# A two-layer recurrent trunk: state-space rotation in PSUM, the skip term on TensorE, GpSimd's tables behind VectorE's, 12 adaLN chunks on VectorE

## The chip, the cores and the metric

The kernel runs on one core of one Trainium2 chip, as one program. The metric is the device time of one execution in microseconds. Everything is float32; the large products of the later stages are made in the fp32r form from a high and a low part of each weight.

## The reference

Two layers over a sequence of 256 tokens of width 2048. Layer 0 mixes tokens with a complex-diagonal state-space layer (S5), layer 1 with a gated recurrent block (RG-LRU); each is followed by a SwiGLU block of width 5632. Six vectors per layer (shift, scale, gate, twice) come from a conditioning vector c by the product with w_ada (adaLN).

```python
cond = silu(c)
for i in range(2):
    mod = cond @ w_ada[i] + b_ada[i]                 # 6 x 2048 numbers
    h = rmsnorm(x, norm_g[i, 0]) * (1 + sc1) + sh1
    y = s5_mixer(h) if i == 0 else rglru_mixer(h)
    x = x + g1 * y
    h = rmsnorm(x, norm_g[i, 1]) * (1 + sc2) + sh2
    x = x + g2 * swiglu(h)
return rmsnorm(x, final_g)

def s5_mixer(h):                                     # 128 groups of 16 channels, 64 complex states each
    u = h @ w_in
    a = exp((lam_re + 1j * lam_im) * dt)             # per group and state
    s[t] = a * s[t-1] + B_bar @ u[t]                 # complex, along the sequence
    y = real(C @ s) + d_skip * u                     # the skip term
    val, gate = split(gelu(y) @ w_glu)
    return val * sigmoid(gate)
```

## The kernel before

**Order.** The program is scheduled by hand: the order of the Python statements is the order on each engine's queue. Tokens are stored in an order in which four neighbours (q = 0 to 3) lie in four blocks of 64, so the scan runs over 64 blocks of four tokens.

**The stream.** All weights come through one list, `items`, into four raw buffers of 1 MB (128 x 2048 float32), loaded by SyncE's queue; `Stream.step` takes the next item and issues loads up to three items ahead, so a load waits for the release of the buffer four items back. An item of kind `f` is used as it is (the S5 input weights `win`); `w` is split by ScalarE into a high part (`wh`, L472) and by VectorE into a low part (`wl`, L487). An item of 128 adaLN columns is worked off in one of two ways, by the string `KINDS`. Kind `p`: TensorE multiplies by the conditioning vector (`ada_p`, L499, four matmuls, eight instructions, four `p` items to a PSUM bank `pa`); behind the fourth, ScalarE copies the row to SBUF (`par`, L505), and TensorE turns it into columns in `rows_out` (`pc`, L520), which are then copied to `modr` (ScalarE in the head, VectorE later). Kind `a`: one VectorE multiply with accumulation over the raw tile and the broadcast vector `cond` (`ada_a`, L491). Before, items 0 to 59 are `p` and 60 to 79 are `a`.

**The head** (`s5_layer`, until the first projection is complete): 32 adaLN items come first. Meanwhile VectorE computes the tables of the state-space layer in `prep`: the step sizes, the powers of a (`ag`, `al`), the decay `dec`, and two tables of eight rotations each (`lo`, `hi`; levels of squaring `cmul`, L164 to L168, `normalise`, L172 to L175, and the table, L249 to L259). GpSimd squares and sums for the norm, and builds with `gen_gl(t)` for a group t of eight S5 groups the matrices `gs` and `ls` (copies L274, products L279, sums L284) from `ag`, `al` and the loaded B and C. `gen2(t)` turns `gs` on TensorE into `G` (transposes L317, copy L318), multiplies `gs` by `ls` into the short convolution `pt` (L326), adds the skip term with a VectorE instruction (L328), and ScalarE copies `pt` into a Toeplitz matrix `T` (`ev`, L332). `gen_p(t)` multiplies out the rotations of a group on VectorE (L295 to L298). In program order `gen_gl(0)` and `gen_gl(1)` stand at steps 7 and 9 of the stream, the scaling of X by the norm (L886) at steps 14 to 17, `gen2(0)` and `gen2(1)` at steps 16 and 21, `gen_p` at steps 22 to 24.

**The loop** runs over t = 0 to 15. Turn t makes the projection of 128 channels on TensorE (L900, 16 k-tiles, 32 instructions) and between its k-tiles the small work of neighbouring turns: the states' inputs `pv` of t - 1 (L358), the outputs `py` of t - 2 (L395, L397), and `gen2(t + 2)`. On VectorE follow `chain` (rotate `pv`, scan, rotate back: L367 to L377) for t - 1 and `gen_p(t + 3)`; on ScalarE the copies `U` (L341), the evictions `T`, the gelu (L923) and `gen_d` (L304); on GpSimd `gen_gl(t + 4)`. When the k-tiles of a `win` item are used up, the stream steps on over the two adaLN items behind it to the next `win`.

After the loop follow the gated product of the S5 layer (`glu`), the SwiGLU block, the LRU layer and the second SwiGLU block. In the LRU layer `x0(j)` makes the products `xb`; `mac` does one k-tile of such a product, with `turn` 1 high part first, and without `turn` low part first.

Of the kernel before, what the change touches and what calls it, by code (L numbers as in the profile page):

```python
# [80 lines left out]
class S5:  # L81
# [4 lines left out]

    def __init__(self, nc, const, far, ps, lam, bcd, ident):
        self.nc, self.const, self.far, self.ps = nc, const, far, ps
        self.lam, self.bcd, self.ident = lam, bcd, ident
        self.work = None  # L90
        self.gt = {}

        def own(nm, a, b, *shape):

            return [(far if i < a else const).tile([P, *shape], F32, name=f"s5{nm}{i}") for i in range(a + b)]

        self.bct = own("bc", 4, 0, 4, 4, 16)

        self.gs = own("gs", 2, 0, 4, 2, 4, 32)

        self.G = own("G", 2, 2, 2, 4, 128) * 4

        self.ls0 = l = own("ls", 2, 4, 4, 2, 5, 32)
        self.ls = [l[i] for i in (0, 1, 2, 3, 4, 5, 0, 1, 2, 3, 4, 5, 0, 2, 3, 4)]

        p = own("pt", 3, 2, 4, 2, 64)
        self.pt = [p[i] for i in (0, 1, 2, 3, 4, 0, 1, 2, 3, 4, 0, 1, 2, 3, 4, 3)]

        self.T0 = t = own("T", 2, 3, 4, 4, 32)
        self.T = 3 * t + [t[2]]  # L110
        self.d0 = own("d0", 0, 2, 8, 64)

    def load(self, w):
        self.lam_t = w.tile([P, 3, 64], F32, name="s5lam")
        self.dsk = self.const.tile([P, 64], F32, name="s5dsk")
        self.nc.sync.dma_start(self.lam_t, self.lam[:, 0:3])
        self.nc.sync.dma_start(self.dsk, self.lam[:, 3])

# [4 lines left out]
    def prep(self, w):  # L123
# [10 lines left out]
        self.ag, self.al, self.lo, self.hi = ag, al, lo, hi  # L134
        self.id4 = c.tile([P, 32], F32, name="s5id")
        for x in self.gs + self.ls0 + self.d0 + self.T0:
            nc.gpsimd.memset(x, 0.0)
        for q in range(4):
            v.tensor_copy(self.id4[32 * q:32 * q + 32], self.ident[32 * q:32 * q + 32, 32 * q:32 * q + 32])

# [64 lines left out]
        cmul(a4, a2, a2)  # L205
        v.tensor_scalar(ag[:, :, 0], ag[:, :, 2], -1.0, None, MUL)
        yield
# [33 lines left out]
        for lev in range(2):  # L241
# [13 lines left out]
            if lev == 0:  # L255
                cmul(e2, p4, p4)
                normalise(e2)
                base = e2
        v.tensor_scalar(hi[:, :, 0], hi[:, :, 2], -1.0, None, MUL)  # L259

    def gen_gl(self, t):
# [44 lines left out]
    def gen2(self, t):  # L306
# [13 lines left out]
        def tt():  # L320

            pt = self.ps.tile([P, 4, 32], F32, tag="pt", bufs=1, name=f"pt{t}")
            tp.append(pt)
            for i in range(2):
                for r in range(4):
                    nc.tensor.matmul(pt[32 * r:32 * r + 32], gs[:, r, i, 3], ls[:, r, i, 0:4], start=(i == 0),  # L326
                                     stop=(i == 1), tile_position=(0, 32 * r), skip_group_check=True)
            nc.vector.scalar_tensor_tensor(pt[:, 0], self.id4, self.dsk[:, 4 * t:4 * t + 1], pt[:, 0], MUL, ADD)  # L328

# [14 lines left out]
    def states(self, t):  # L344
# [15 lines left out]
        def chain():  # L360
            vv, d0 = st["pv"], self.d0[t % 2]

            def wt(nm):
                return w.tile([P, 4, 2, 64], F32, tag=nm, bufs=1, name=f"{nm}_{t}")
            m, n = wt("sm"), wt("sn")
            co, si = (bc(pt[:, :, i], 2, 2) for i in range(2))
# [3 lines left out]
            v.tensor_tensor(m[:, :, 1], m[:, :, 1], n[:, :, 0], SUB)  # L370
            v.tensor_tensor_scan(n.rearrange("p r i n -> p (r i n)"), d0.rearrange("p a n -> p (a n)"),
                                 m.rearrange("p r i n -> p (r i n)"), 0.0, MUL, ADD)
            S = w.tile([P, 4, 2, 64], F32, tag="S", bufs=2, name=f"S_{t}")
            v.tensor_tensor(m, n, si, MUL)
            v.tensor_tensor(S, n, co, MUL)
            v.tensor_tensor(S[:, :, 0], S[:, :, 0], m[:, :, 1], SUB)
# [31 lines left out]
class Stream:  # L408
# [105 lines left out]
    def rows_out(self):  # L514

        if self.rows:
            nc, (rows, n) = self.nc, self.rows
            pc = self.ps.tile([P, 4], F32, tag="pc", bufs=1, name=f"pc{n}")
            for j in range(4):
                nc.tensor.matmul(pc[:, j:j + 1], rows[:, j * P:j * P + P], self.ones, start=True, stop=True)  # L520
            self.cols(self.mod[:, n - 3:n + 1], pc)
            self.rows = None
# [53 lines left out]
class Model:  # L576
# [250 lines left out]
    def s5_layer(self):  # L827
# [3 lines left out]
        with ExitStack() as c:  # L831
# [3 lines left out]
            far = tc.tile_pool(name="s5far", bufs=1, side="right")  # L835
            s5 = S5(nc, const, far.__enter__(), s5ps, d["s5lam"], d["s5bc"], self.ident)
            hf = const.tile([P, 16, T], F32, name="s5h")
# [17 lines left out]
            with tc.tile_pool(name="s5prep", bufs=1) as pw:  # L855
# [9 lines left out]
                stat = self.norm_stat(mm, "s5")  # L865
                for i in range(14):
                    st.step()
# [5 lines left out]
                    if 1 <= i < 4:  # L873
                        for k in range(6 * i - 6, min(6 * i, 16)):
                            self.sq_add(k, nc.gpsimd)
                    if i in (7, 9):
                        s5.gen_gl((i - 7) // 2)
                for _ in prep:
                    pass
            next(stat, None)  # L880
            s5.work = c.enter_context(tc.tile_pool(name="s5w", bufs=1))
            for i in range(14, 28):
                st.step()
                if i < 18:
                    for k in range(4 * i - 56, 4 * i - 52):
                        nc.vector.tensor_tensor(self.X[:, k], self.X[:, k], self.rs, MUL)  # L886
                if i in (16, 21):
                    for f in s5.gen2((i - 16) // 5):
                        f()
                    s5.gen_gl((i - 16) // 5 + 2)  # L890
                if 22 <= i < 25:
                    s5.gen_p(i - 22)
            st.late = True
# [164 lines left out]
    def lru_layer(self):  # L1058
        nc, tc, d = self.nc, self.tc, self.d
        v, s, e = nc.vector, nc.scalar, nc.gpsimd  # L1060
        with ExitStack() as c:
# [112 lines left out]
            def x0(j):  # L1174
                if j > 1:
                    first.append(self.product(ps, self.rhs_h, 16, f"xb{j}", "evict", (1,) if j % 4 == 2 else ()))

# [59 lines left out]
    def run(self):  # L1237
# [50 lines left out]
        items += ada(12, 16) + ada(28, 29) + win[0:1] + ada(29, 32)  # L1288
        items += mix(win[1:], ada(32, 60), 2)
        items += mix(wglu, ada(60, 80), 2, 3, 2) + gu[0][0][:2] + ada(80, 84) + mix(gu[0][0][2:], ada(84, 96), 1, 3)  # L1290
# [9 lines left out]
        self.st.ps = ctx.enter_context(tc.tile_pool(name="side", bufs=1, space=PSUM))  # L1300
        self.st.ew = const
        self.s5_layer()
        self.ps = ctx.enter_context(tc.tile_pool(name="mm", bufs=4, space=PSUM))
# [26 lines left out]

KINDS = "p" * 60 + "a" * 20 + "qqqp" + "a" * 56 + "qqqp" + "a" * 32 + "qqqp" + "a" * 12

# [13 lines left out]
def lay_out(i):  # L1346
# [37 lines left out]
    ldt = np.broadcast_to(i["s5_log_dt"][0][:, None], (P, 64))  # L1384
    dsk = np.repeat(i["s5_d"][0].reshape(16, P).T, 4, axis=1)
    o["s5lam"] = np.stack([states(i["s5_lam_re"][0]), states(i["s5_lam_im"][0]), states(ldt), dsk], 1)
# [43 lines left out]
```

## Time and profile before

| | |
|---|---|
| time, median of 3 runs | 2495.81 us (2494.57 to 2498.04) |
| the profiled execution's own time | 2500.8 us |
| its span, granted clock | 2499.0 us, 0.976 |
| PE busy, PEld busy | 2379.5 us (95%), 2045.1 us (82%) |
| DVE, ACT, POOL busy | 1895.4 us (76%), 1298.4 us (52%), 339.3 us (14%) |
| read from HBM | 614.57 MB, 247 GB/s over the span |

PE is TensorE's matmul, PEld its weight load, DVE is VectorE, ACT ScalarE, POOL GpSimd, SP SyncE. L12 is line 12 of the kernel. A line of the timeline has the start and the length in us, the engine, the line of the kernel, the operation, out<-in and a count, and in brackets the idle time before it and what ended it. A group has its busy time, the mean of one instruction in ns, and the idle time of the engine just before its instructions. Matmuls are pipelined and their ends modelled, so that a busy PE need not be PE at its peak.

### The profile page before, as it was taken

Reading aid. Unit: us, or ns where it says so; the run is one execution under the profiler, and the core shown is the slowest. Engines: PE = TensorE matmul, PEld = TensorE weight load, DVE = VectorE, ACT = ScalarE, POOL = GpSimd, SP = SyncE. Lnnn points to the kernel's source line nnn. Section 1 sums busy time; section 2 is a strip of 40 time slices with the busy share of each in tenths; the row PEclk is TensorE's granted clock in tenths of the full one; section 3 lists DMA queues with packets and bytes.
Section 4 is the critical chain, followed back from the end, with each engine's and each line's share of the span. In section 5 each row is a group of like instructions: output and inputs, shape, how many; then the busy total and the mean of one; then the engine's idle time right before and its main releaser. Section 6 shows DMA issues by size and latency. Waiting matters only on the chain. (4 is left out here: it accounts for less than half of the span.)

```text
span 2499.0 us, 37144 instructions
## 1 busy us (share of the span) xinstructions
PE 2379.5 (95%) x14374; PEld 2045.1 (82%) x14374; DVE 1895.4 (76%) x2618; ACT 1298.4 (52%) x2525; POOL 339.3 (14%) x345
## 2 busy tenths in 40 slices
PE   5389998999999999999999898999999999999998
PEld 1167787887888888888888787888788888888887
DVE  9857757888776887777989999898777555555565
ACT  1257785456455444444456765554645444444443
POOL 5558730001000000000002332010100000000000
PEclk8689998999999999999999999999999999999999
DMA  9465555887666898776985446879776456555453
GB/s 374 184 237 211 211 211 224 325 321 284 251 255 236 287 337 314 291 296 241 326 319 195 149 169 236 331 273 334 282 299 253 171 186 215 202 187 198 168 191 135
DMA packets 98416, 619.07 MB, mean 248 GB/s; under 512 B 11200, under 2 KB 15680, under 8 KB 38976
## 3 DMA queue, kind: packets, MB, share of 16 engines
q1 hardware_dynamic: 96368, 613.04, 66.7%
q10 hardware_dynamic: 1872, 3.67, 0.4%
q8 instruction: 112, 1.84, 0.3%
q14 instruction: 64, 0.52, 0.1%
HBM read 614.57 MB, written 2.10 MB: 247 GB/s over the span
## 5 line engine op out<-in xcount | busy, mean ns | idle before, releaser
L487 DVE TENSOR_TENSOR wl<-raw,wh 128x1024 fp32r<-128x1024 f32 (+2 forms) x824 | 887.0, 1099 | 337.6 <-ACT wh L472 335.2
L472 ACT ACTIVATE wh<-raw 128x1024 fp32r<-128x1024 f32 (+2 forms) x824 | 768.4, 952 | 659.6 <-PE d L605 186.8
L605 PE MATMUL u<-H,wh 128*128 128x512 f32 x1376 | 472.0, 389 | 0.0
L605 PE MATMUL d<-hid,wh 128*128 128x512 f32 x1376 | 469.3, 389 | 0.0
L605 PE MATMUL g<-H,wh 128*128 128x512 f32 x1328 | 455.7, 389 | 0.0
L604 PE MATMUL d<-hid,wl 128*128 128x256 f32 x1376 | 380.1, 276 | 0.0
L604 PE MATMUL u<-H,wl 128*128 128x256 f32 x1376 | 379.8, 276 | 0.0
L604 PE MATMUL g<-H,wl 128*128 128x256 f32 x1328 | 366.7, 276 | 0.0
L605 PEld LDWEIGHTS u<-H,wh 128*128 128x128 f32 x1376 | 258.3, 188 | 53.6
L605 PEld LDWEIGHTS d<-hid,wh 128*128 128x128 f32 x1376 | 258.3, 188 | 53.1
L605 PEld LDWEIGHTS g<-H,wh 128*128 128x128 f32 x1328 | 249.3, 188 | 50.8
L491 DVE CUSTOM_DVE_ANT_0 raw<-raw,cond 128x2048 f32<-128x2048 f32 x120 | 274.7, 2290 | 3.6 <-DMA raw<-in_wada 3.6
L604 PEld LDWEIGHTS d<-hid,wl 128*128 128x128 f32 x1376 | 258.3, 188 | 0.6
L604 PEld LDWEIGHTS u<-H,wl 128*128 128x128 f32 x1376 | 258.3, 188 | 0.0
L604 PEld LDWEIGHTS g<-H,wl 128*128 128x128 f32 x1328 | 249.2, 188 | 0.9
L499 PE MATMUL pa<-raw,condz 128*32 128x512 f32 x576 | 87.5, 714 | 70.7 <-ACT par L505 45.6
L900 PE MATMUL in<-s5h,raw 128*128 128x256 f32 x512 | 145.1, 401 | 1.3 <-ACT s5h L854 1.3
L793 ACT ACTIVATE gs<-gs 128x256 f32<-128x256 f32 x88 | 36.7, 418 | 202.8 <-DVE gs L642 202.8
L605 PE MATMUL lg<-H,wh 128*128 128x512 f32 x340 | 118.1, 394 | 0.0
L605 PE MATMUL xb<-H,wh 128*128 128x512 f32 x315 | 110.9, 395 | 0.0
L499 PEld LDWEIGHTS pa<-raw,condz 128*32 128x32 f32 x576 | 14.8, 118 | 110.9 <-ACT par L505 52.8
L900 PEld LDWEIGHTS in<-s5h,raw 128*128 128x128 f32 x512 | 87.9, 195 | 19.6 <-issue 11.1
(419 smaller groups left out, 3761.3 us busy)
## 6 DMA issues: line engine op xcount, KB each, us to landing
raw<-in_wada SPq DMA_DIRECT2D x192, 1024.0 KB, 6.0
raw<-in_gu SPq DMA_DIRECT2D x176, 1024.0 KB, 4.8
raw<-in_dn SPq DMA_DIRECT2D x128, 704.0 KB, 4.2
raw<-in_lruin SPq DMA_DIRECT2D x44, 1024.0 KB, 5.0
raw<-in_s5glu SPq DMA_DIRECT2D x32, 1024.0 KB, 6.2
raw<-in_lruout SPq DMA_DIRECT2D x32, 704.0 KB, 5.6
raw<-in_s5win SPq DMA_DIRECT2D x16, 1024.0 KB, 8.5
raw<-in_lruri SPq DMA_DIRECT2D x8, 512.0 KB, 5.4
```

The costliest lines, as they stand in the source:

```text
L472: nc.scalar.activation(dh, src, AF.Copy)
L487: self.nc.vector.tensor_tensor(*self.lazy.pop(0), SUB)
L491: self.nc.vector.tensor_tensor_reduce(t, t, self.cond, 1.0, 0.0, MUL, ADD, self.mod[:, n:n + 1])
L499: nc.tensor.matmul(self.bank[32 * c:32 * c + 32], self.condz[:, 4 * q + c], t[:, 512 * c:512 * c + 512], start=(q == 0), stop=(q == 3), ti ...
L604: mm(bank[:, 0], wl, x[:, 0], start=first, stop=False, skip_group_check=True)
L605: mm(bank, wh, x, start=False, stop=last, skip_group_check=True)
L793: nc.scalar.activation(g, g, AF.Silu)
L900: nc.tensor.matmul(bank, st.next()[0], hf[:, k], start=(k == 0), stop=(k == 15))
```

## The change

It has five parts. (1) `gen_gl(0)` and `gen_gl(1)` follow all of `prep`, `gen2(0)` and `gen2(1)` move to steps 23 and 27 of the stream, `gen_p` to steps 23 to 25, the scaling of X to steps 16 to 19; three negations of tables move to the end of `prep`. (2) The skip term is a table `skip` (identity blocks times `d_skip`, 128 x 512, built once by VectorE), and TensorE adds it to `pt` with four small matmuls against the identity; L328 goes. `pt` moves into one PSUM bank with `pc`, (3) which makes room for a bank `px`: `chain` keeps its product m there instead of in SBUF, and the scan writes over `pv` in PSUM. (4) adaLN items 48 to 59 become kind `a`; behind each of the `win` items 1 to 12 now stand one `p` and one `a`, behind 13 and 14 two `p`. (5) All `xb` products take the first k-tile high part first, not only every fourth.

```diff
@@ S5.load, S5.prep @@
-        self.dsk = self.const.tile([P, 64], F32, name="s5dsk")
+        self.dsk = w.tile([P, 16], F32, name="s5dsk")
...
+        self.skip = self.far.tile([P, 16, 32], F32, name="s5skip")
...
+        v.tensor_tensor(self.skip, bc(id4, 1, 16), bc(self.dsk, 2, 32), MUL)
...
-        v.tensor_scalar(ag[:, :, 0], ag[:, :, 2], -1.0, None, MUL)
...
-        v.tensor_scalar(al[:, :, 2], al[:, :, 0], -1.0, None, MUL)
...
         v.tensor_scalar(hi[:, :, 0], hi[:, :, 2], -1.0, None, MUL)
+        v.tensor_scalar(ag[:, :, 0], ag[:, :, 2], -1.0, None, MUL)
+        v.tensor_scalar(al[:, :, 2], al[:, :, 0], -1.0, None, MUL)
@@ S5.gen2, tt @@
-            pt = self.ps.tile([P, 4, 32], F32, tag="pt", bufs=1, name=f"pt{t}")
+            pt = self.pct[:, 4:].rearrange("p (a b) -> p a b", b=32)
...
-                                     stop=(i == 1), tile_position=(0, 32 * r), skip_group_check=True)
-            nc.vector.scalar_tensor_tensor(pt[:, 0], self.id4, self.dsk[:, 4 * t:4 * t + 1], pt[:, 0], MUL, ADD)
+                                     stop=False, tile_position=(0, 32 * r), skip_group_check=True)
+            for r in range(4):
+                nc.tensor.matmul(pt[32 * r:32 * r + 32, 0], self.ident[:, 32 * r:32 * r + 32], self.skip[:, t],
+                                 start=False, stop=True, tile_position=(0, 32 * r), skip_group_check=True)
@@ S5.states, chain @@
-            m, n = wt("sm"), wt("sn")
+            m = self.ps.tile([P, 4, 2, 64], F32, tag="px", bufs=1, name=f"px{t}")
+            n = w.tile([P, 4, 2, 64], F32, tag="sn", bufs=1, name=f"sn_{t}")
...
-            v.tensor_tensor_scan(n.rearrange("p r i n -> p (r i n)"), d0.rearrange("p a n -> p (a n)"),
+            v.tensor_tensor_scan(vv.rearrange("p r i n -> p (r i n)"), d0.rearrange("p a n -> p (a n)"),
                                  m.rearrange("p r i n -> p (r i n)"), 0.0, MUL, ADD)
...
-            v.tensor_tensor(m, n, si, MUL)
-            v.tensor_tensor(S, n, co, MUL)
+            v.tensor_tensor(m, vv, si, MUL)
+            v.tensor_tensor(S, vv, co, MUL)
@@ Model.s5_layer @@
-                for i in range(14):
+                for i in range(16):
                     st.step()
...
-                    if i in (7, 9):
-                        s5.gen_gl((i - 7) // 2)
...
-            for i in range(14, 28):
+            s5.gen_gl(0)
+            s5.gen_gl(1)
+            for i in range(16, 28):
                 st.step()
-                if i < 18:
-                    for k in range(4 * i - 56, 4 * i - 52):
+                if i < 20:
+                    for k in range(4 * i - 64, 4 * i - 60):
                         nc.vector.tensor_tensor(self.X[:, k], self.X[:, k], self.rs, MUL)
-                if i in (16, 21):
-                    for f in s5.gen2((i - 16) // 5):
+                if i in (23, 27):
+                    for f in s5.gen2((i - 23) // 4):
                         f()
-                    s5.gen_gl((i - 16) // 5 + 2)
-                if 22 <= i < 25:
-                    s5.gen_p(i - 22)
+                    s5.gen_gl((i - 23) // 4 + 2)
+                if 23 <= i < 26:
+                    s5.gen_p(i - 23)
@@ Model.lru_layer, x0 @@
-                    first.append(self.product(ps, self.rhs_h, 16, f"xb{j}", "evict", (1,) if j % 4 == 2 else ()))
+                    first.append(self.product(ps, self.rhs_h, 16, f"xb{j}", "evict", (1,)))
@@ Model.run @@
-        items += mix(win[1:], ada(32, 60), 2)
+        both = [x for p, a in zip(ada(32, 44), ada(48, 60)) for x in (p, a)]
+        items += mix(win[1:], both + ada(44, 48), 2)
...
+        pct = self.st.ps.tile([P, 132], F32, name="pct")
+        self.st.pc, self.pct = pct[:, 0:4], pct
@@ module @@
-KINDS = "p" * 60 + "a" * 20 + "qqqp" + "a" * 56 + "qqqp" + "a" * 32 + "qqqp" + "a" * 12
+KINDS = "p" * 48 + "a" * 32 + "qqqp" + "a" * 56 + "qqqp" + "a" * 32 + "qqqp" + "a" * 12
```

More of the change, by code (lines that the diff above doesn't have):

```diff
@@ L81, with __init__ @@
 class S5:
-    def __init__(self, nc, const, far, ps, lam, bcd, ident):
+    def __init__(self, nc, pct, const, far, ps, lam, bcd, ident):
+        self.pct = pct
         self.nc, self.const, self.far, self.ps = nc, const, far, ps
@@ L114, in load @@
         self.lam_t = w.tile([P, 3, 64], F32, name="s5lam")
-        self.dsk = self.const.tile([P, 64], F32, name="s5dsk")
+        self.dsk = w.tile([P, 16], F32, name="s5dsk")
         self.nc.sync.dma_start(self.lam_t, self.lam[:, 0:3])
-        self.nc.sync.dma_start(self.dsk, self.lam[:, 3])
+        self.nc.sync.dma_start(self.dsk, self.lam[:, 3, 0:16])
     def load_bc(self, t):
@@ L134, in prep @@
         self.ag, self.al, self.lo, self.hi = ag, al, lo, hi
-        self.id4 = c.tile([P, 32], F32, name="s5id")
+        id4 = w.tile([P, 32], F32, name="s5id")
+        self.skip = self.far.tile([P, 16, 32], F32, name="s5skip")
         for x in self.gs + self.ls0 + self.d0 + self.T0:
@@ L138, in prep @@
         for q in range(4):
-            v.tensor_copy(self.id4[32 * q:32 * q + 32], self.ident[32 * q:32 * q + 32, 32 * q:32 * q + 32])
+            v.tensor_copy(id4[32 * q:32 * q + 32], self.ident[32 * q:32 * q + 32, 32 * q:32 * q + 32])
+        v.tensor_tensor(self.skip, bc(id4, 1, 16), bc(self.dsk, 2, 32), MUL)
         def one(nm):
@@ L361, in chain @@
             vv, d0 = st["pv"], self.d0[t % 2]
-            def wt(nm):
-                return w.tile([P, 4, 2, 64], F32, tag=nm, bufs=1, name=f"{nm}_{t}")
-            m, n = wt("sm"), wt("sn")
+            m = self.ps.tile([P, 4, 2, 64], F32, tag="px", bufs=1, name=f"px{t}")
+            n = w.tile([P, 4, 2, 64], F32, tag="sn", bufs=1, name=f"sn_{t}")
             co, si = (bc(pt[:, :, i], 2, 2) for i in range(2))
@@ L517, in rows_out @@
             nc, (rows, n) = self.nc, self.rows
-            pc = self.ps.tile([P, 4], F32, tag="pc", bufs=1, name=f"pc{n}")
+            pc = self.pc
             for j in range(4):
@@ L835, in s5_layer @@
             far = tc.tile_pool(name="s5far", bufs=1, side="right")
-            s5 = S5(nc, const, far.__enter__(), s5ps, d["s5lam"], d["s5bc"], self.ident)
+            s5 = S5(nc, self.pct, const, far.__enter__(), s5ps, d["s5lam"], d["s5bc"], self.ident)
             hf = const.tile([P, 16, T], F32, name="s5h")
@@ L1384, in lay_out @@
     ldt = np.broadcast_to(i["s5_log_dt"][0][:, None], (P, 64))
-    dsk = np.repeat(i["s5_d"][0].reshape(16, P).T, 4, axis=1)
+    dsk = np.tile(i["s5_d"][0].reshape(16, P).T, (1, 4))
     o["s5lam"] = np.stack([states(i["s5_lam_re"][0]), states(i["s5_lam_im"][0]), states(ldt), dsk], 1)
```

## The prediction

> **What bounds the kernel now.** I looked first at the spans: one core, 2499.0 us at a mean granted clock of 0.976. The 40 slices show PE at nine tenths everywhere but in the first three slices, so I went to the waits, the busiest groups, and then to stretches of 20 us at the start. The waits are written as waiter, what it waited for, total us, times, longest.
>
> ```profile
> ACT s5T L332 <- DVE pt L328: 32.5, 1, 32.5
> PE pa L499 <- ACT par L505: 45.6, 6, 32.9
> DVE sm L367 <- PE pv L358: 60.9, 14, 9.1
> ```
>
> The stretches give from:to, length, busy us of PE, PEld, DVE, ACT, POOL, then granted clock, DMA share and GB/s.
>
> ```profile
> 0.00:20.00 20.00, 5.81 (x24) 0.64 (x24) 18.27 (x36) 1.60 (x3) 12.39 (x21) 1.00 0.87 343
> 20.00:40.00 20.00, 12.08 (x68) 3.35 (x72) 18.86 (x53) 7.80 (x21) 10.17 (x14) 0.90 0.89 353
> 40.00:60.00 20.00, 16.48 (x84) 6.18 (x84) 19.04 (x51) 1.54 (x4) 8.65 (x11) 0.67 1.01 419
> 60.00:80.00 20.00, 7.21 (x56) 3.15 (x56) 19.58 (x27) 1.19 (x2) 19.01 (x23) 0.76 0.72 291
> 80.00:100.00 20.00, 0.00 (x0) 0.00 (x0) 18.68 (x51) 1.88 (x8) 5.29 (x5) 0.50 0.00 0
> 145.00:368.00 223.00, 221.54 (x1625) 176.61 (x1626) 153.33 (x186) 177.19 (x725) 152.85 (x144) 0.99 0.53 205
> ```
>
> Until 60 us the head streams at DMA speed. Between 80 and 100 us neither PE nor DMA does anything. One wait explains it: gen2(0)'s skip term (L328) stands on VectorE behind all of prep and the scaling of X; ScalarE's T evictions (L332) wait 32.5 us for it; the eviction of the adaLN row (par) is queued behind those; PE waits 32.9 us for par, the four raw buffers fill, and the DMA stops. From 145 to 368 us, the state-space loop, PE is busy 221.5 of 223 us. There VectorE waits for PE: 60.9 us in 14 waits, 4.35 us per turn. So the head is a chain of waits and the loop is PE-bound. The timeline of the head (start, us, engine, line):
>
> ```profile
> 50.91 0.39 DVE L164 TENSOR_TENSOR prm<-b 128x128 f32<-128x128 f32 x1
> 52.76 2.51 POOL L279 TENSOR_TENSOR gm<-s5bc,s5al 128x640 f32<-128x640 f32 x2
> 60.35 2.03 POOL L284 TENSOR_TENSOR s5gs<-gm,gm 64x384 f32<-64x384 f32 x2
> 62.44 0.66 PE L317 MATMUL pg<-ident,s5gs 128*128 128x128 f32 x4 [3.00 <-POOL s5gs L284]
> 62.45 1.14 POOL L274 COPY s5gs<-s5bc 64x64 f32<-64x64 f32 x4
> 64.83 1.94 PE L499 MATMUL pa<-raw,condz 128*32 128x512 f32 x8
> 71.84 2.19 POOL L284 TENSOR_TENSOR s5gs<-gm,gm 64x384 f32<-64x384 f32 x2
> 86.77 0.38 DVE L164 TENSOR_TENSOR prm<-p 128x128 f32<-128x128 f32 x1
> 89.32 0.11 DVE L249 MEMSET s5hi<- 128x64 f32 x1
> 93.44 0.43 DVE L259 TENSOR_SCALAR s5hi<-s5hi 128x512 f32<-128x512 f32 x1
> 98.04 3.82 ACT L332 ACTIVATE s5T<-pt 32x128 f32<-32x128 f32 x16 [32.51 <-DVE pt L328]
> 101.95 0.59 ACT L505 ACTIVATE par<-pa 128x512 f32<-128x512 f32 x1
> 122.45 2.08 ACT L854 ACTIVATE s5h<-X,mod,gscs 128x256 f32<-128x256 f32 x4 [0.35 <-DVE gscs L845]
> 133.77 1.09 ACT L854 ACTIVATE s5h<-X,mod,gscs 128x256 f32<-128x256 f32 x2 [9.25 <-DVE gscs L845]
> 134.35 5.76 PE L900 MATMUL in<-s5h,raw 128*128 128x256 f32 x16
> 140.04 1.07 PE L499 MATMUL pa<-raw,condz 128*32 128x512 f32 x8
> 145.09 1.02 PE L900 MATMUL in<-s5h,raw 128*128 128x256 f32 x2 [1.28 <-ACT s5h L854]
> ```
>
> **The change, part 1: the head.** The last row is my yardstick: with the 13th k-tile of the first projection, at 145.09 us, the head is over.
>
> VectorE first. At 50.91 us the low table begins; GpSimd starts its first group at 52.76, and from then VectorE creeps. Its own pace shows at the end, when GpSimd is idle: a square and a normalisation of the power take 89.32 - 86.77 = 2.55 us, a table 93.44 - 89.32 = 4.12. A level is two of the first and one of the second, 9.22. The rest of prep (low level, one square, high level) is then 9.22 + 2.55 + 9.22 = 21.0 us instead of 42.5, and ends at 71.9; with L259's 0.43 and some 0.7 for the new 128x512 skip table (the size of L375 below) at 73.0. The negations of ag and al only move.
>
> GpSimd next. It may start its products only now. Group 0 took it 52.76 to 62.38, 9.6 us; group 1 with its copies 62.45 to 74.03, 11.6. Both ran beside VectorE, as they will again (gen_p now falls here), so I take these: gs(0) is ready at 73.0 + 9.6 = 82.6 and gs(1) at 94.2.
>
> The DMA meanwhile: 20 x (343 + 353 + 419) = 22.3 MB by 60 us; X, the B and C groups and small loads are 2.8 of it by their shapes, so 18.6 of the 1.05 MB tiles are in. The head needs 33 (32 adaLN, one win). The other 14.4 at 419 GB/s, 2.50 us each, are in at 96 us if nothing stops them. Tile 23 is in at 74, so PE waits at gen2(0) until 82.6, some 7 us, while the four buffers fill; at most 2 us of DMA are lost. gen2(0) takes 64.83 - 62.44 = 2.4, four chunks and a column row about 6: 91. At gen2(1) PE waits again, for gs(1), until 94.2, and is through at 96.6. In both places par now precedes gen2 in ScalarE's queue, and the evictions wait for PE alone; nothing on VectorE's queue is in front of them.
>
> From there: T evictions 3.8 us, then gen_d, which I put at 0.6, and six of L854, 2.08 + 1.09: into(0..7) starts at about 104.2. The rest of the head took 145.09 - 134.35 = 10.7 us. So 115 instead of 145: **-30 us**. Bounds: if GpSimd were no wait at all, the last chunk would be in at 96 and 145.09 - 140.04 = 5.1 us remain: 101 to 102, -43. If VectorE did not speed up without GpSimd, prep would end at 94 and everything behind it 21 us later than above: -9. I take -30 because every duration in it has been measured in the same neighbourhood.
>
> Past the head GpSimd's groups 2 and 3 would end at about 105 and 115 us; gen2(2) wants the first at 115 and gen2(3) the second at about 119. No new wait, but little margin.
>
> **Part 2: the loop.** Rows of the timeline, the first and last of 13 starts of a turn, one pair of adaLN chunks, one column row, one toeplitz product:
>
> ```profile
> 162.26 1.35 SPq L444 DMA_DIRECT2D raw<-in_wada  x2
> 239.33 1.92 PE L499 MATMUL pa<-raw,condz 128*32 128x512 f32 x16
> 253.20 0.64 PE L326 MATMUL pt<-s5ls,s5gs 128*32 128x128 f32 x16
> 256.25 1.05 PE L520 MATMUL pc<-ones,par 128*128 128x1 f32 x8
> 347.63 1.35 SPq L444 DMA_DIRECT2D raw<-in_wada  x2
> ```
>
> A turn is (347.63 - 162.26) / 12 = 15.45 us. PE loses 12 chunks, 12 x 0.96 = 11.5 us, and three column rows, 3 x 1.05 = 3.2. It gains the skip term: four matmuls, eight instructions, half of the 16 in the toeplitz row and with fewer columns, so at most 0.32 us; in 14 turns 4.5. Net 11.5 + 3.2 - 4.5 = **-10 us**. For the skip term the far ends are 0 (hidden under its neighbours) and, with full-width weight loads as in other lines, some 8 x 0.19 = 1.5 us or 21 us in all; its stationary is 32 columns wide like the toeplitz one, so I stay with that row.
>
> Does VectorE let PE go faster? Groups (busy, mean ns, idle before) and single lines (ns min/median/max):
>
> ```profile
> L491 DVE CUSTOM_DVE_ANT_0 raw<-raw,cond 128x2048 f32<-128x2048 f32 x120 | 274.7, 2290 | 3.6 <-DMA raw<-in_wada 3.6
> L377 DVE TENSOR_TENSOR S<-S,sm 128x256 f32<-128x256 f32 x16 | 16.5, 1032 | 0.0
> L377 DVE TENSOR_TENSOR S<-S,sm x16: 415/1498/1505, 164.5 to 391.5; 128x256 f32<-128x256 f32 x16
> L375 DVE TENSOR_TENSOR S<-sn,s5pt x16: 678/720/722, 163.5 to 390.5; 128x512 f32<-128x512 f32 x16
> L367 DVE TENSOR_TENSOR sm<-pv,s5pt x16: 680/691/692, 157.4 to 386.5; 128x512 f32<-128x512 f32 x16
> L284 POOL TENSOR_TENSOR s5ls<-gm,gm x32: 1527/1862/1902, 55.3 to 328.2; 64x640 f32<-64x640 f32 x32
> L604 PE MATMUL xb<-H,wl 128*128 128x256 f32 x315 | 88.7, 282 | 0.0
> L605 PEld LDWEIGHTS xb<-H,wh 128*128 128x128 f32 x315 | 60.0, 190 | 12.3
> L604 PE MATMUL lg<-H,wl 128*128 128x256 f32 x340 | 95.0, 279 | 4.7 <-DVE wl L487 4.7
> ```
>
> L377, two SBUF operands, costs 0.415 us alone and 1.5 beside GpSimd; L367, one operand in PSUM, costs 0.68 to 0.69 every time. With the rotation in PSUM, L377 falls by 1.03 - 0.42 = 0.6 us per turn and its neighbours a little; L328 goes to PE. Against that a turn gains an adaLN chunk, 2.29 us alone and up to 2.29 + 1.90 if it first sits out one GpSimd instruction. VectorE needs 15.45 - 4.35 = 11.1 us per turn now, then 12.8 to 14.7, and PE 15.45 - 0.96 + 0.32 - 0.2 = 14.6. It just fits, the more so as the chunk follows the chain directly and may start while GpSimd is at its copies. ScalarE is busy 177 of 223 us, 12.3 per turn, and loses three par copies: it fits.
>
> [...]
>
> **Part 3: the rest.** The xb products open with the high part: 15 of them swap two matmuls. PE never waits for wl in xb (0.0), so 0; the one wait nearby, 4.7 us at lg, is the end below, and one exposed weight load of 0.19 us per product, +3 us, the end above. The smaller skip load, the shared PSUM bank for pc and pt, and the SBUF moves cost nothing that a row shows: pt's readers finish on ScalarE in a turn's first half, pc is written at its end.
>
> Sum: -30 - 10 = -40 us on a profiled execution of 2500.8 us (span 2499.0). The median shown is 2495.81, 0.2% lower; -40 from it is **2456 us**.
>
> **The rivals.** (A) GpSimd's late start becomes the new wait: groups 0 and 1 stretch beside X's scaling and gen_p, and gen2(2) and gen2(3) wait at the loop's door. For it: the groups end only 4 to 10 us before they are wanted. Against: GpSimd idles between groups now. At 6 us per late group for two groups the gain is 28: 2468. (B) The loop keeps its 15.45 us because VectorE fills the turn: only the head's gain, 2466. For it: 14.7 against 14.6. (C) Slower: VectorE becomes the loop's bound outright. The raw buffer of an adaLN chunk on VectorE is freed by VectorE, and the win tile two turns on is loaded into it, so a late VectorE also starves PE. To eat the head's 30 us in 12 turns a turn must reach 15.45 + 2.5 = 17.9 us, 5.1 above the 12.8: each chunk would sit out about three GpSimd instructions. Then 2500 and more; 17.9 us is the point from which it decides. Against it: L377 never takes longer than 1.505, one instruction's wait. [...] (D) The stall only changes its owner: PE waits as long for gs as it did for par, gain below 5 us: 2493. Against: GpSimd had gs(1) ready 21 us after 52.76. (E) More: GpSimd never in the way in the head, -43 - 10 = -53: 2443.
>
> **How the numbers follow.** Forecast 50% (2448 to 2464), A 17%, B 16%, E 7%, C 6%, D 4%. The range takes the forecast, A, B and half of E: 2443 to 2478. A measurement here tells changes beyond 0.2%, 5 us. Faster: the forecast, A, B, E and part of D, 0.91; same: 0.03; slower: C, 0.06.
>
> **What would show it.** Right: no stretch without PE and DMA near 80 to 100 us; L259 at about 72 us; two waits of pg for gs of 3 to 8 us; the 13th k-tile at 110 to 120 us; turns of about 14.7 us; L377 at 0.42 throughout; L367's idle before it shrinking from 4.35 to 1 or 2 us but not gone. Wrong: the chunk's mean above 4 us, PE idle before py or in, win tiles landing late, or L259 still past 85 us.

## The result, and the profile after

The changed kernel takes 2457.91 us (median, 2456.33 to 2458.86) against 2495.19 us (2491.30 to 2498.04): ratio 0.985, 95% interval 0.984 to 0.986, 37 us less. Its profiled execution has a span of 2456.3 us at a granted clock of 0.977. The forecast was 2456 us, -40 from the median of before.

Three marks cut a trace into pieces: the start of the 13th k-tile of the first projection (the prediction's yardstick for the head), the start of the first gate tile (`glu`), and the second k-tile of the first product `v` of the SwiGLU block (L604 before, L610 after). The loop lies between the first and the second mark, the gate's start between the second and the third.

| profiled execution | head ends | loop | gate's start | the rest | span |
|---|---|---|---|---|---|
| before | 145.1 | 229.9 | 33.0 | 2091.0 | 2499.0 |
| after | 111.3 | 216.5 | 38.9 | 2089.6 | 2456.3 |
| difference | -33.8 | -13.4 | +5.9 | -1.4 | -42.7 |

Both rows are single executions. The one of before took 2500.8 us, 5.6 above the median, so its pieces add up to a larger difference (42.7 us) than the medians show (37).

The stretches of after, with the columns of the prediction's fence:

```profile
60.00:80.00 20.00, 12.45 (x57) 3.38 (x58) 19.50 (x50) 1.37 (x3) 10.94 (x9) 0.63 1.02 421
80.00:100.00 20.00, 15.54 (x121) 7.04 (x120) 9.28 (x10) 10.28 (x39) 19.13 (x22) 0.69 0.74 270
111.00:325.00 214.00, 212.06 (x1647) 176.65 (x1648) 166.51 (x197) 180.58 (x727) 153.03 (x147) 1.00 0.58 221
```

The stretch from 80 to 100 us, in which neither PE nor DMA moved, is gone: 15.5 us of PE, 270 GB/s. In the loop PE is as full as before (212.06 of 214 us). The head's timeline of after:

```profile
67.66 0.43 DVE L261 TENSOR_SCALAR s5hi<-s5hi 128x512 f32<-128x512 f32 x1
76.96 2.72 POOL L288 TENSOR_TENSOR s5gs<-gm,gm 64x384 f32<-64x384 f32 x2
79.74 1.11 PE L321 MATMUL pg<-ident,s5gs 128*128 128x128 f32 x4 [4.08 <-POOL s5gs L288]
92.29 1.12 PE L321 MATMUL pg<-ident,s5gs 128*128 128x128 f32 x4 [0.94 <-POOL s5gs L288]
99.96 1.05 PE L526 MATMUL pct<-ones,par 128*128 128x1 f32 x8 [2.33 <-ACT s5T L338]
111.33 0.70 PE L906 MATMUL in<-s5h,raw 128*128 128x256 f32 x2 [1.96 <-ACT s5h L860]
```

The last instruction of prep's tables starts at 67.7 instead of 93.4 us; the two groups' `gs` end at 79.7 and 92.2, and PE waits for each, the second time under one microsecond. In the loop, two loads of a `win` item four turns apart, then groups from 120 to 325 us, then single lines (ns min/median/max):

```profile
146.49 0.33 SPq L450 DMA_DIRECT2D raw<-in_s5win  x1
203.60 0.33 SPq L450 DMA_DIRECT2D raw<-in_s5win  x1
...
L497 DVE CUSTOM_DVE_ANT_0 raw<-raw,cond 128x2048 f32<-128x2048 f32 x12 | 33.2, 2767 | 0.0
L373 DVE TENSOR_TENSOR px<-pv,s5pt 128x512 f32<-128x512 f32 x14 | 9.8, 700 | 40.7 <-PE pv L364 40.7
...
L383 DVE TENSOR_TENSOR S<-S,px x16: 414/414/416, 127.7 to 345.4; 128x256 f32<-128x256 f32 x16
L288 POOL TENSOR_TENSOR s5ls<-gm,gm x32: 1527/1707/3488, 71.2 to 281.8; 64x640 f32<-64x640 f32 x32
```

A turn is (203.60 - 146.49) / 4 = 14.28 us; most turns with a column row take 15.2. L383 (L377 before, up to 1505 ns) takes 414 ns every time. VectorE still waits for PE ahead of the chain. The adaLN chunk costs 2.77 us on average, and one of GpSimd's sums now takes up to 3.49 us, where it never exceeded 1.90.

### The profile page after: what moved, and what is told of

It is laid out like the page before. It is cut to its first block, busy times and chain, and to the rows that moved or that the text cites. A ratio compares the mean times of both kernels' runs of the same rounds, so it can differ in the third digit from the quotient of the medians.

```text
span 2456.3 us, 37129 instructions
## 1 busy us (share of the span) xinstructions
PE 2369.6 (96%) x14382; PEld 2042.3 (83%) x14382; DVE 1883.3 (77%) x2624; ACT 1297.8 (53%) x2522; POOL 335.7 (14%) x345
## 5 line engine op out<-in xcount | busy, mean ns | idle before, releaser
L610 PE MATMUL u<-H,wl 128*128 128x256 f32 x1376 | 379.9, 276 | 0.0
L610 PE MATMUL d<-hid,wl 128*128 128x256 f32 x1376 | 379.9, 276 | 0.0
L610 PE MATMUL g<-H,wl 128*128 128x256 f32 x1328 | 366.8, 276 | 0.0
L497 DVE CUSTOM_DVE_ANT_0 raw<-raw,cond 128x2048 f32<-128x2048 f32 x132 | 308.0, 2334 | 1.7 <-DMA raw<-in_wada 1.5
L610 PEld LDWEIGHTS d<-hid,wl 128*128 128x128 f32 x1376 | 258.3, 188 | 0.6
L610 PEld LDWEIGHTS u<-H,wl 128*128 128x128 f32 x1376 | 258.3, 188 | 0.0
L610 PEld LDWEIGHTS g<-H,wl 128*128 128x128 f32 x1328 | 249.3, 188 | 1.0
L505 PE MATMUL pa<-raw,condz 128*32 128x512 f32 x480 | 80.3, 766 | 26.8 <-DMA raw<-in_wada 21.9
L611 PE MATMUL xb<-H,wh 128*128 128x512 f32 x300 | 103.8, 391 | 0.0
L610 PE MATMUL lg<-H,wl 128*128 128x256 f32 x340 | 95.5, 281 | 4.8 <-DVE wl L493 4.8
```

Source lines behind the costliest of these rows:

```text
L497: self.nc.vector.tensor_tensor_reduce(t, t, self.cond, 1.0, 0.0, MUL, ADD, self.mod[:, n:n + 1])
L505: nc.tensor.matmul(self.bank[32 * c:32 * c + 32], self.condz[:, 4 * q + c], t[:, 512 * c:512 * c + 512], start=(q == 0), stop=(q == 3), ti ...
L610: mm(bank[:, 0], wl, x[:, 0], start=first, stop=False, skip_group_check=True)
L611: mm(bank, wh, x, start=False, stop=last, skip_group_check=True)
```

## The experiments

Each experiment is the changed kernel with one edit; `order_only` alone is the kernel before with one. Ratios are against the kernel before on the same chip; the marks are those of the table above.

| kernel | median us | ratio, 95% interval | head ends | loop | gate's start |
|---|---|---|---|---|---|
| order_back | 2464.5 | 0.988 (0.986 to 0.990) | 119.7 | 216.5 | 35.7 |
| order_only | 2466.0 | 0.988 (0.986 to 0.990) | 113.3 | 230.6 | 33.3 |
| groups_early | 2463.3 | 0.987 (0.985 to 0.988) | 116.4 | 216.5 | 35.7 |
| skip_vector | 2459.7 | 0.986 (0.984 to 0.987) | 114.9 | 222.1 | 35.2 |
| chunks_tensor | 2471.9 | 0.991 (0.989 to 0.992) | 117.8 | 232.0 | 36.4 |
| rotation_sbuf | 2494.4 | 0.999 (0.998 to 1.000) | 117.7 | 241.0 | 42.0 |
| both_back | 2479.5 | 0.993 (0.992 to 0.995) | 117.5 | 229.5 | 42.3 |
| no_groups | 2467.1 | 0.988 (0.986 to 0.990) | 117.4 | 216.6 | 42.1 |
| xb_back | 2458.7 | 0.985 (0.984 to 0.986) | 116.4 | 216.6 | 35.0 |
| bank_free | 2457.5 | 0.984 (0.983 to 0.986) | 117.4 | 216.5 | 36.0 |
| more_chunks | 2457.4 | 0.985 (0.983 to 0.986) | 117.7 | 214.0 | 37.6 |
| more_bank | 2456.1 | 0.983 (0.982 to 0.985) | 117.8 | 214.0 | 38.2 |

### The head: two cures for one stall

order_back restores the head's old order (groups at steps 7 and 9, gen2 at 16 and 21), and keeps all else:

```diff
+                    if i in (7, 9):
+                        s5.gen_gl((i - 7) // 2)
...
-            s5.gen_gl(0)
-            s5.gen_gl(1)
-            for i in range(16, 28):
+            for i in range(14, 28):
...
-                if i in (23, 27):
+                if i in (16, 21):
```

> The changed kernel with the old order of the head (GpSimd's groups 0 and 1 at steps 7 and 9, gen2 at steps 16 and 21, the scaling of X at 14 to 17); skip term on TensorE, rotation in PSUM, chunks and xb as changed. Theory: two things held the old head, ScalarE's wait for L328 and VectorE slowed down by GpSimd. Only the first is gone here, so the tables still end at about 94 us instead of 68, and gen_p, the modulation and the 13th k-tile follow late: k-tile at 118 to 124 us instead of 111, time about 2467 (2464 to 2471). Rival: the wait for L328 was all, and the order adds nothing: 2458.

order_only applies the new order of the head to the kernel before, and nothing else; the skip term stays on VectorE:

```diff
-                    if i in (7, 9):
-                        s5.gen_gl((i - 7) // 2)
...
+            s5.gen_gl(0)
+            s5.gen_gl(1)
...
-                if i in (16, 21):
+                if i in (23, 27):
```

> The kernel before with the new order of the head and nothing else: skip term on VectorE, rotation in SBUF, no chunks moved. Theory: the order alone gives nearly all of the head's 34 us, because gen2's VectorE instruction then stands behind nothing but the scaling of X, done by 74 us: 13th k-tile at 111 to 115 us, loop as before: 2462 (2459 to 2466). Rival: with the skip term still on VectorE its wait only moves, now behind gen_p, and ScalarE and PE wait as before: gain under 15, 2480 or more.

groups_early puts back only the start of the two groups; gen2 stays late:

```diff
+                    if i in (7, 9):
+                        s5.gen_gl((i - 7) // 2)
...
-            s5.gen_gl(0)
-            s5.gen_gl(1)
```

> The changed kernel with GpSimd's groups 0 and 1 put back in front of the later tables (steps 7 and 9, and the negations they need at their old places); gen2, the scaling of X and gen_p stay at their new steps. Theory: GpSimd and VectorE hold each other up while both work on two SBUF operands; the tables end at about 90 us again, gen2(0) has no wait, but VectorE's gen_p and modulation come late, 13th k-tile at about 117 us: 2464 (2461 to 2468). Rival: once gen2 is moved, GpSimd's place is worth nothing or costs, as PE no longer waits for gs (5.0 us in the changed kernel): 2453 to 2458.

The end of prep and the waits of PE from 60 to 125 us, in order_back, then in order_only:

```profile
97.04 0.43 DVE L263 TENSOR_SCALAR s5hi<-s5hi 128x512 f32<-128x512 f32 x1
62.66 3.81 ACT L338 ACTIVATE s5T<-pct 32x128 f32<-32x128 f32 x16
PE in L906 <- ACT s5h L860: 7.9, 2, 6.6
```

```profile
70.59 0.43 DVE L257 TENSOR_SCALAR s5hi<-s5hi 128x512 f32<-128x512 f32 x1
PE pg L317 <- POOL s5gs L284: 8.2, 2, 4.9
```

All three came out as the theory had it. With the old order prep is as slow as ever (97 us), but the 32.5 us stall is gone all the same: the evictions of T, at 98.04 before, start at 62.66, since the skip term no longer stands in VectorE's queue. What is left of prep's lateness is one wait of 6.6 us for `s5h` at the first projection. So either half removes most of the stall: the order alone brings the head to 113.3, the skip term alone to 119.7, both to 111.3 to 117.8. Of the 37 us, the order is worth about 6.6 (medians 2464.5 against 2457.9) once the skip term is on TensorE; the intervals of the two ratios meet at 0.986, so this figure is rough. In groups_early prep reaches that last instruction at 90.4 and the group tables are no wait, but PE waits 9.5 us for `s5h`.

### The loop: what pays for the chunks

skip_vector gives the skip term back to VectorE (in `pct`):

```diff
-                nc.tensor.matmul(pt[32 * r:32 * r + 32, 0], self.ident[:, 32 * r:32 * r + 32], self.skip[:, t],
-                                 start=False, stop=True, tile_position=(0, 32 * r), skip_group_check=True)
+            nc.vector.tensor_tensor(pt[:, 0], pt[:, 0], self.skip[:, t], ADD)
```

> The changed kernel with the skip term added by VectorE again (one 128x32 add from the same table in the place of the four matmuls). Theory: eight instructions of 0.24 us a turn leave PE and VectorE, which has 1.65 us of idle left per turn, takes 0.25: 3 us faster if evictions do not wait, 2455 (2452 to 2458). Rival: the add queues behind the chain and an adaLN chunk on VectorE, ScalarE's evictions and behind them PE wait for it: 2460 to 2475.

Loads of `win` three turns apart, and the waits of PE from 125 to 330 us:

```profile
151.10 0.33 SPq L448 DMA_DIRECT2D raw<-in_s5win  x1
193.76 0.33 SPq L448 DMA_DIRECT2D raw<-in_s5win  x1
PE pct L524 <- DVE pct L332: 3.3, 3, 1.4
```

Neither theory holds whole. An ordinary turn is 42.66 / 3 = 14.22 us, 0.06 less than with the matmuls, so eight small matmul instructions cost 0.06 us a turn and not the 0.32 of the prediction. But the column rows share a PSUM tile with `pt` and now wait for VectorE's addition: from the first product of a turn to that of the next, three turns with a row take 16.6 us, where after has 15.2, 15.2 and 16.05. One turn without a row takes 15.9 us: the granted clock was 0.51 in it from 266.0 to 269.5 us. The loop is 5.6 us longer.

chunks_tensor puts items 48 to 59 back on TensorE:

```diff
-KINDS = "p" * 48 + "a" * 32 + "qqqp" + ...
+KINDS = "p" * 60 + "a" * 20 + "qqqp" + ...
```

> The changed kernel with adaLN items 48 to 59 back on TensorE in the old sequence of items. Theory: PE sets the turn; 12 chunks of about 0.9 us and three column rows of 0.9 come back: loop 216.5 to about 229 us, time 2470 (2467 to 2473). Rival: VectorE with its chunk was already as long as PE, so that taking it off gives back more than half: loop at most 223, 2463.

The loop grows by 15.5 us, to 232.0, the time by 14: the time as the theory had it, the loop 3 us longer than its 229.

rotation_sbuf puts the product and the scan of `chain` back in SBUF:

```diff
-            m = self.ps.tile([P, 4, 2, 64], F32, tag="px", bufs=1, name=f"px{t}")
+            m = w.tile([P, 4, 2, 64], F32, tag="sm", bufs=1, name=f"sm_{t}")
...
-            v.tensor_tensor_scan(vv.rearrange(...
+            v.tensor_tensor_scan(n.rearrange(...
...
-            v.tensor_tensor(m, vv, si, MUL)
-            v.tensor_tensor(S, vv, co, MUL)
+            v.tensor_tensor(m, n, si, MUL)
+            v.tensor_tensor(S, n, co, MUL)
```

> The changed kernel with the rotation back in SBUF (m and the scan's result as before); everything else as changed. Theory: VectorE has 24.6 us of idle in 12 turns, 2.05 a turn; the SBUF forms cost it 1.2 us more per turn and GpSimd up to as much; the turns of 14.28 us stay or grow by at most 0.3, and the last pv no longer waits for the end of the chain (2 to 3 us back): 2455 to 2461, loop (13th k-tile to the start of glu) 216 to 221 us. Rival: the rotation in PSUM is what makes room for the adaLN chunks; without it VectorE is the bound and a turn grows by 1 us: loop 228, time 2468 or more.

Groups of VectorE and waits of PE from 120 to 325 us, then a piece of one turn (start, us, engine):

```profile
L497 DVE CUSTOM_DVE_ANT_0 raw<-raw,cond 128x2048 f32<-128x2048 f32 x12 | 37.3, 3108 | 0.0
L381 DVE TENSOR_TENSOR S<-sn,s5pt 128x512 f32<-128x512 f32 x12 | 16.4, 1367 | 0.0
L383 DVE TENSOR_TENSOR S<-S,sm 128x256 f32<-128x256 f32 x12 | 14.0, 1164 | 0.0
L373 DVE TENSOR_TENSOR sm<-pv,s5pt 128x512 f32<-128x512 f32 x12 | 8.3, 692 | 17.7 <-PE pv L364 17.0
PE py L403 <- DVE S L383: 6.2, 5, 1.2
PE py L403 <- DVE S L382: 4.3, 5, 1.5
...
183.42 1.77 DVE L381 TENSOR_TENSOR S<-sn,s5pt 128x512 f32<-128x512 f32 x1
185.22 1.39 DVE L382 TENSOR_TENSOR S<-S,sm 128x256 f32<-128x256 f32 x1
186.53 1.75 DVE L383 TENSOR_TENSOR S<-S,sm 128x256 f32<-128x256 f32 x1
188.21 3.62 DVE L497 CUSTOM_DVE_ANT_0 raw<-raw,cond 128x2048 f32<-128x2048 f32 x1
183.03 3.29 POOL L283 TENSOR_TENSOR gm<-s5bc,s5al 128x640 f32<-128x640 f32 x2
186.40 3.28 POOL L288 TENSOR_TENSOR s5ls<-gm,gm 64x640 f32<-64x640 f32 x2
```

My theory fell, and its rival was right by far: without the rotation in PSUM the whole change is worth nothing (0.999, 0.998 to 1.000). In that piece the operations that read two SBUF tiles and GpSimd's beside them both stretch: L381 takes 1.77 us, L382 1.39 and L383 1.75, against 0.68, 0.42 and 0.41 in after, and GpSimd's two products take 3.29 us and its two sums 3.28, where one of each takes 1.27 and 1.53 at its shortest in after. PE waits for S, and the loop is 241.0 us, longer than before the change. PE's waits are not all of it: in this loop PE is idle for 14.7 us in all, and the granted clock was 0.50 from 188.4 to 202.0 us and from 243.0 to 246.4, with PE busy throughout; in the loop of after it was not below 1.00. The raw buffers come free later too (SyncE waits 80.1 us for the chunks, 40.5 in after), but no wait of PE here is for a load. Two experiments separate the parts. both_back makes this edit and the one of chunks_tensor together:

> The changed kernel with two edits undone at once: the rotation on SBUF tiles as before, and the twelve chunks back on TensorE. Each undone alone cost 36 us (rotation) and 14.5 us (chunks). Theory: the two costs are one, VectorE's turn. A chunk on VectorE and a rotation that reads and writes SBUF alone both stretch when GpSimd builds its tables beside them; without the chunks the rotation has 4 us of room in each turn and costs nothing of the period. Loop (13th k-tile to the first gate tile) 231 to 234 us, as with the chunks undone alone (232.0), time 2470 to 2475. Rival: the rotation in SBUF costs the period by itself, through TensorE waiting for S; then the costs add, loop about 256 us and time about 2508.

no_groups leaves out GpSimd's groups from the seventh on, so that its later turns multiply by tables of earlier groups, and is otherwise rotation_sbuf:

```diff
-        if t >= 16:
+        if t >= 6:
             return
```

> The rotation on SBUF tiles with twelve chunks on VectorE, as in the run that came out at 2494 us, but GpSimd's table groups are left out from the seventh group on (later turns multiply by tables of earlier groups). That leaves GpSimd idle in the loop from its third turn. Theory: the 36 us came from VectorE and GpSimd holding each other up; with GpSimd idle a chunk takes 2.2 us instead of 3.27, the multiplies of the chain 0.7 instead of 1.0 to 1.35, the turn comes back to 14.3 and the loop to 216 to 221 us; time 2456 to 2463. Rival: VectorE's own work with the rotation in SBUF is longer than the turn even alone (the instructions are longer in SBUF whoever is beside them); the loop stays above 230 us and the time above 2474.

Groups of VectorE in no_groups from 120 to 325 us, and a wait of PE at the gate's start:

```profile
L497 DVE CUSTOM_DVE_ANT_0 raw<-raw,cond 128x2048 f32<-128x2048 f32 x12 | 28.5, 2376 | 0.0
L373 DVE TENSOR_TENSOR sm<-pv,s5pt 128x512 f32<-128x512 f32 x14 | 9.7, 692 | 69.8 <-PE pv L364 69.7
L381 DVE TENSOR_TENSOR S<-sn,s5pt 128x512 f32<-128x512 f32 x14 | 9.6, 687 | 0.0
...
PE v L603 <- DVE gg L986: 5.4, 1, 5.4
```

The loop settles it. Four kernels differ only in these two parts: with the rotation in PSUM, 232.0 us with the chunks on TensorE and 216.5 with them on VectorE; with the rotation in SBUF, 229.5 and 241.0. The chunks give 15.5 us with the rotation in PSUM and cost 11.5 without it. With GpSimd idle the rotation in SBUF is as good as the one in PSUM: 216.6. So it is the two engines at the SBUF together, not VectorE's own work. The times of both_back and no_groups are above what I expected (2479.5 for 2470 to 2475, 2467.1 for 2456 to 2463), and the surplus lies behind the loop: in the three kernels without the `px` tile, `v` waits 5.4 us for the gate's last read (`gg`), and the gate's start takes 42 us instead of 35 to 39. I take it that the PSUM pools behind it lie on other banks then; that was not tried.

### The gate's start, and two kernels beyond the change

xb_back restores part 5 (only every fourth `xb` product high part first):

```diff
-"evict", (1,)))
+"evict", (1,) if j % 4 == 2 else ()))
```

> The changed kernel with the xb products in their old form (only every fourth opens high part first). Theory: PE never waits for the low part there, nothing changes: 2458 within 1.5 us; xb's start to lg's start 170 to 172 us as in all runs. Rival: the order spares a wait on VectorE per product and its loss costs 3 to 5 us.

From the first `xb` to the first `lg` the traces have 171.1 us before, 170.8 after and 170.9 here: the edit is worth nothing.

The gate's start takes longer after the change than before. In after, PE stops after eight gate matmuls, at 329.6 us; here are its next work, the VectorE instruction that ends just then, and the next steps of 5 us:

```profile
336.57 3.65 PE L364 MATMUL pv<-U,s5G 128*128 128x64 f32 x16 [6.98 <-ACT H L652]
335.75 0.68 DVE L381 TENSOR_TENSOR S<-pv,s5pt 128x512 f32<-128x512 f32 x1
...
337.00:342.00 5.00, 5.00 (x22) 4.75 (x22) 4.27 (x11) 0.16 (x1) 0.00 (x0) 0.50 0.01 3
342.00:347.00 5.00, 5.00 (x24) 4.86 (x23) 3.71 (x7) 0.00 (x0) 0.00 (x0) 0.50 0.00 0
347.00:352.00 5.00, 5.00 (x19) 4.42 (x19) 0.00 (x0) 3.86 (x18) 0.00 (x0) 0.50 0.00 0
```

The profile names ScalarE's H, but `pv` doesn't read H, and its input U was complete at 334.9; L381, which ends at 336.4, is the last reader of `pv`, which the scan now overwrites, so the next `pv` waits for the chain up to there. Behind the pause the granted clock is 0.50 for 15 us in which PE never rests. Before the change the same place reads:

```profile
380.20 0.63 PE L358 MATMUL pv<-U,s5G 128*128 128x64 f32 x4 [3.46 <-ACT U L341]
...
380.00:385.00 5.00, 4.24 (x18) 3.87 (x19) 4.86 (x11) 4.17 (x16) 0.00 (x0) 0.59 0.40 170
385.00:390.00 5.00, 5.00 (x32) 4.68 (x31) 4.90 (x11) 0.00 (x0) 0.00 (x0) 0.73 0.01 3
```

There the pause is 3.5 us instead of 7.0, and the clock is at 0.50 for 6.8 us (380.9 to 387.7). bank_free writes the scan of tile 14 alone to SBUF, so that the bank comes free after the second product:

```diff
-            v.tensor_tensor_scan(vv.rearrange(...
+            z = n if t == 14 else vv
+            v.tensor_tensor_scan(z.rearrange(...
```

> The changed kernel with one exception: the chain of group 14 scans into SBUF (n) instead of over pv. Theory: the 7 us wait of PE before the last pv, put down to ScalarE, is for the PSUM bank that VectorE's chain now holds until its second rotation is read (336.43 us, pv starts at 336.57); with the bank free early, pv of group 15 starts 2.5 to 3.5 us sooner and TensorE's clock falls less: glu's first product 2.5 to 6 us shorter, 2453 (2451 to 2456). Rival: the wait is for ScalarE's copies U and the splits, as the profile says: 2458.

```profile
339.21 1.66 PE L364 MATMUL pv<-U,s5G 128*128 128x64 f32 x6 [3.48 <-ACT U L347]
343.26 0.56 PE L611 MATMUL glu<-H,wl 128*128 128x256 f32 x1
...
344.00:349.00 5.00, 5.00 (x22) 4.66 (x21) 4.90 (x11) 0.00 (x0) 0.00 (x0) 0.50 0.02 3
349.00:354.00 5.00, 5.00 (x21) 4.61 (x21) 2.14 (x5) 2.65 (x13) 0.00 (x0) 0.50 0.00 0
```

The wait is shown to be for the bank: `pv` starts 5.2 us after the first gate tile (333.97) instead of 8.7, and the gate tiles go on 9.3 us after it (343.26) instead of 12.1. The gain is not there: PE then works at a granted clock of 0.50 until 355, and the gate's start is 36.0 us, within the 35.0 to 38.9 of the kernels that hold the bank. All five experiments on the changed kernel in which the wait for this `pv` is the short one (the three with the rotation in SBUF and the two with the bank free) spend about 16 us at 0.50 behind it; of the seven with the bank held, after does too (15.4), and the other six spend 5 to 8. An early `pv` alone doesn't explain it: in before and in order_only it starts as early (5.2 us after the first gate tile), and the clock is at 0.50 for 6.8 us. What decides it is not settled; in after PE was busy in all of the 15.4 us.

more_chunks gives VectorE four more items, 44 to 47, in the last turns, where GpSimd has no more groups to build:

```diff
-KINDS = "p" * 48 + "a" * 32 + "qqqp" + ...
+KINDS = "p" * 44 + "a" * 36 + "qqqp" + ...
```

> The changed kernel with four more chunks (44 to 47) on VectorE instead of TensorE. They stand in the last turns of the loop, where GpSimd has no table left to build. Theory: TensorE is the loop's bound there as in the turns before, four chunks of 0.9 us and one set of rows of 0.9 us go from its path, 4.5 us: loop 212 us, time 2453 to 2454 (0.2 per cent less). Rival: the last turns end on VectorE's chain, whose U and S the gate stage waits for, and a chunk of 2.2 us ahead of the chain sends it later: what the loop gives, the wait at the gate's start takes back, time 2456 to 2460.

more_bank joins it with the edit of bank_free:

> The changed kernel with two edits on top: four more chunks (44 to 47) on VectorE, and the scan of the last but one chain (tile 14) written to the SBUF tile, so that the PSUM bank of pv comes free after the second product. With the first alone the loop was 214.0 us and the first gate tiles 37.6 us, of which TensorE waited 7.5 us for that bank. Theory: the two do not hide each other now, pv(15) starts 3 us sooner after the loop's end, the gate tiles take 34 to 35 us; time 2453 to 2455. Rival: whatever TensorE waits less at the gate's start, the clock that it is granted behind the pause takes back, as when the bank alone was freed; gate tiles 36 us or more, time 2456 to 2459.

Both rivals were right. The loop gets 2.5 us shorter, not 4.5, and the gate's start takes it back: 37.6 us, and 38.2 with the bank free, again behind a pause (7.5 and 3.7 us) and at a granted clock of 0.50. more_bank has the lowest median, 2456.1 us, ratio 0.983 (0.982 to 0.985), but its interval overlaps that of after; neither is shown to be better than the changed kernel.

## Why the prediction was right

**Head, -30 forecast, -33.8 in the trace of after.** The last table instruction of prep (72 forecast, 67.7), gs(0) (82.6, 79.7), gs(1) (94.2, 92.2) and the yardstick (115, 111.3) all came a few microseconds sooner, and the two waits for gs were 4.1 and 0.9 instead of 3 to 8 each. The surplus is an execution's luck at the very start. Here are VectorE's four small copies, in after and in xb_back, which is the same program up to there, and GpSimd's last memsets in xb_back:

```profile
1.37 5.17 DVE L141 COPY s5id<-ident 32x32 f32<-32x32 f32 x4
```

```profile
1.37 12.22 DVE L141 COPY s5id<-ident 32x32 f32<-32x32 f32 x4
10.61 2.39 POOL L139 MEMSET s5T<- 128x512 f32 x5
```

In xb_back, as in the trace of before, the first of VectorE's copies takes 11.65 us and ends with the string of GpSimd's memsets, at 13.0 us; in after all four are over at 6.5 us, while the memsets run on to 13.4. The last table instruction then starts at 71.8 to 72.1, and the yardstick stands at 115 to 118 in the nine experiments with the new head and this start: close to the 115 forecast. Against before, which had this start too, the head's gain is then 27 to 30 us. Starting the copies ahead of the memsets would be the next edit for the head; it was not tried. What the step did not see is that the two edits cure the same stall: it gave the -30 to the order and to the skip term together, and order_back, with prep at 97 us, has still 25 us of the head's gain (some 4 of them by the same luck, an estimate: its copies took 6.3 us, and in after the early copies brought prep's last instruction from 72 to 67.7). The bound of -9, for a VectorE that does not speed up under the new order, is tested by no run: where prep was slow, GpSimd's groups didn't wait for it.

**Loop, -10 forecast, -13.4 measured.** The mean turn, from the adaLN loads at 141.65 and 300.48 us, is 158.83 / 11 = 14.4 us for 14.6 (14.28 is a turn without a column row). The skip term was sized too high, 0.32 us per turn by the toeplitz row for 0.06; the chunks and their rows gave 15.5 for the 14.7 forecast. That L383 would be 0.42 throughout, and that VectorE would keep some room, held: it waits 24.6 us in 12 turns ahead of the chain,

```profile
DVE px L373 <- PE pv L364: 24.6, 12, 6.4
```

so it needs 14.4 - 2.05 = 12.4 us per turn, below the 12.8 to 14.7 forecast. (Over the whole loop the waits are longer, 40.7 us in 14, 2.9 each, for 4.35 before.) A PSUM operand also cost no more than the prediction's rows had it (L367 680 to 692 ns from PSUM, L375 678 at its shortest from SBUF): L381 takes 681 ns from PSUM and 687 from SBUF without GpSimd. But the step put the rotation's worth at 0.6 us per turn of an engine off the path. Its real worth is that of the whole loop: 24.5 us (the half clock in rotation_sbuf's loop included), since without it the chunks turn the sign.

**The gate's start, nothing forecast, +5.9 measured** (+2.0 to +3.4 in five other executions with the rotation in PSUM and the bank held, +4.6 in more_chunks). This is the term that the sum lacks: a head that ends 30 us sooner and a loop 13 us shorter don't change the gate, but the scan over `pv` holds a bank that had come free after two products: PE's wait there is 7.0 us instead of 3.5. In the five executions the clock behind it is much as before, and this wait is what they show, some 2 to 3 us. The clock is a second part: bank_free has the short wait and the long stretch at 0.50, and its gate's start is still 3.0 us longer than before. after has both; xb_back, the same program up to there, has the short stretch (5.5 us), so the long one in after is chance in part. Why the clock stays down longer is open. -30 - 10 missed by -3.8, -3.4 and +5.9, which partly cancel.

**The rest.** xb: 0, as forecast. The shared bank was to cost nothing: in the head the column rows wait for the evictions of T, 3.5 us in two waits, 2.33 of them in the fence of the head above; in the loop nothing that before does not have.

**The rivals.** A (late groups as a new wait): at the loop's door PE waits for no group. B (VectorE fills the turn): no. D (the stall only changes its owner): PE waits 5.0 us for gs in all, not 32.9. E (no wait for GpSimd in the head): the two waits for gs stand. C, VectorE as the loop's bound, is no part of this kernel, but it is what rotation_sbuf runs into. Its argument against was that an instruction sits out one of GpSimd's at most; the first copy above, 11.65 us long, ended only with a whole string of them. In the loop of after the operand's place shows: L373, L381 and L383, each with one operand in PSUM, keep their length to 10 ns (693 to 700, 680 to 681, 414 to 416), while the chunk, which has two SBUF inputs, takes 2.77 us on average where it takes 2.28 at its shortest, and GpSimd's sums, 1.53 us at their shortest, take up to 3.49 beside it.

## What to carry to other kernels

Price an edit with its partners, not alone: moving twelve chunks to VectorE was worth -15.5 or +11.5 us in the loop, by where the operands of its neighbours lie. For L381 the operand in PSUM was worth little beside an idle GpSimd (0.68 us, 0.69 in SBUF) and much beside a busy one (0.68 us, 1.37 in SBUF). Where two edits act on one chain of waits, undo each by itself before you credit either. And a tile that is overwritten in place is held longer (the last `pv` started 8.7 us after the first gate tile in after, 5.2 in bank_free): ask who waits for it where the pipeline drains.

## What the runs showed of the hardware that I had not expected

- A VectorE copy of 32 x 32 numbers, which started 0.1 us behind GpSimd's memsets, ended only after all of them in ten of the fourteen traces: 11.65 us for the first in the trace of before, 12.22 for the four in xb_back. In order_only the four took 10.8 us, in order_back 6.3, in after and groups_early 5.2.
- The granted clock behind a pause of 3.5 to 7.5 us stayed at 0.50 for 5 to 16 us in which PE was busy almost throughout. A shorter pause did not mean a shorter stretch: behind 3.5 to 3.7 us it was 6.8 us in two traces and about 16 in five.
- Eight matmul instructions with a stationary of 32 columns, set between others, cost 0.06 us a turn: 14.28 us against 14.22 in skip_vector, and 15.14 in chunks_tensor against 15.08 in order_only.
